# A second pair as seven products, with its sums stored early and another pair's sums made by transfers

## The chip, the cores and the metric

The kernel runs on one core of a Trainium2 chip. The metric is the time of one execution on the device in microseconds (us). Engines are named PE (TensorE, matmuls), PEld (TensorE's weight loads), DVE (VectorE), ACT (ScalarE), POOL (GpSimd) and SP (SyncE, which issues most transfers).

## What is computed

One decoder layer on 512 tokens of width 1024, all in float32: attention with forget gates, a residual with layer norm, a gated MLP with a causal convolution of three taps, a second residual with layer norm, and a gated embedding of 256 values per token.

```python
mix = fox_mixer(x, attn_w_in[j], attn_b_f[j], attn_w_out[j])
x = layer_norm(DEEPNORM_ALPHA * x + mix, ln_mix_g[i], ln_mix_b[i])
ffn = conv_ffn(x, ffn_w_up[i], ffn_conv_w[i], ffn_conv_b[i], ffn_w_down[i])
x = layer_norm(DEEPNORM_ALPHA * x + ffn, ln_ffn_g[i], ln_ffn_b[i])
gate = jax.nn.sigmoid(x @ ple_w_gate[i] + ple_b_gate[i])
x = x + gate * (p[i] @ ple_w_proj[i])
...
def conv_ffn(x, w_up, conv_w, conv_b, w_down):
    u, g = jnp.split(x @ w_up, [FFN_DIM], axis=-1)
    g = causal_dwconv(g, conv_w, conv_b)
    return (jax.nn.gelu(g, approximate=False) * u) @ w_down
```

The change lies in the MLP's first matrix product, `x @ w_up`, with 2 x 2816 output columns: 22 blocks of 128 for `g` and as many for `u`.

## The kernel before, in words

**Three matmuls for one.** Each float32 operand is cut into a high part, rounded to the matmul's type, and a low part, the rest. A product of two operands is the sum of three matmuls: high by high, high by low, low by high (`three`, L151). So a product of 128 x 1024 weights with 512 tokens is 8 row blocks of 3 matmuls, 24 in all.

**Weight units.** All weights pass through the class `Weights`, 128 x 1024 values at a time, called units, in the order in which they were added. A unit is loaded by SP into one of four `raw` tiles (or a spare part of the tile `side`, at places that a small loop fixes, L353 to 359); ACT makes its high part `whi` (L130); DVE makes its low part `wlo` by subtracting (L136). For units with `by_dma`, ACT instead writes the negated high part into `wlo` (L132), and POOL issues a transfer that adds the weights from DRAM to what lies there (L133). Pairs `whi` and `wlo` rotate in five places (`SPLIT_BUFS`), so the cut of a unit waits until TensorE is done with the one five back. A product asks for its unit with `get`, which also cuts up to four units ahead.

**Pairs.** The 22 blocks of features are worked through as eleven pairs, numbered 0 to 10. A plain pair (0, 1 and 10 before) is four products of 24 matmuls with 512 columns: `g` and `u` of each of its two blocks. A pair of seven products (`UP_PAIRS`) treats the 2 x 2 blocks of weights (two halves of the rows, two blocks of columns) by Strassen's scheme in Winograd's form: seven products of a quarter's size in place of eight, for `g` and `u` each, all with 256 columns (half of the tokens). `up_step` runs them in four steps, each for `g` and then for `u`: steps 0 to 2 have 24 matmuls a side, step 3 has 12. Steps 1 and 2 need sums of the weights' blocks and sums of the MLP's input, `xs`, which `x_sums` makes when pair 0 ends (L879 to 886). In step 0 ACT copies a half of the bank out and fills it with zeros (L913, L914), and step 1 adds to it; after step 1 ACT copies results into `E` (L922 to 925), after step 2 DVE subtracts (L929), and the convolution, Gelu and product of each block follow (L855 to 864).

**Where the weights' sums come from.** For `KEPT` pairs DVE makes them during the attention phase, and they are stored in DRAM as `kept` (`keep_load`, `keep_sums`, L544 to 547). For the pair in `IN_DRAM` the weights are copied to `kept` early (`up_copies`), and eight transfers of 256 KB that add within DRAM make the sums (`sums_beside`): ACT writes one value (L320), POOL copies it (L321) and issues the transfer (L322), one at each place that `BESIDE` names for a pair. After them come 16 such transfers for the sums of the last stage's gate weights. For the other pairs, 2 and 9, DVE makes the sums as their units arrive (L215, L216, L223, L237).

**Order.** From pair 1 on, ACT and DVE run in the order in which the code is written (`manual_schedule`). Each of the first three groups of three pairs is followed by its part of the second matrix product, spread over the pairs of the next group; pairs 0 to 2 have no such work beside them.

Of the kernel before, what the change touches and what calls it, by code (L numbers as in the profile page):

```python
# [12 lines left out]
AF = mybir.ActivationFunctionType  # L13
# [3 lines left out]
P = 128  # L17
# [13 lines left out]

CHUNKS = (None,) + ((1,) * 8 + (0, 1, 2, 1),) * 2 + ((1, 1, 2, 1, 2, 2, 2, 1),)

UP_PAIRS = (2, 3, 4, 5, 6, 7, 8, 9)

KEPT = (3, 4, 5, 6, 7)

IN_DRAM = (8,)

BESIDE = {2: (0, 2, 3), 3: (0, 2, 3), 4: (0, 2, 3), 5: (0, 2), 6: (0, 2, 3), 7: (0, 2), 8: (0, 2, 3),  # L40
          9: (0, 2, 3), 10: (0, 2)}

DMA_PAIRS = (1, 2)

APART = (2, 3, 4, 5, 6, 7, 8, 9)
HALF = S // 2
ALPHA = 2.0 ** 0.25
EPS = 1e-5
# [9 lines left out]
RAW_BUFS = 4  # L58

COPIES = (2, 3)  # L60

BANKS = ("six", "six", "two", "six", "six", "six", "two", "six")
SPLIT_BUFS = 5
# [86 lines left out]
def trunk_layer(ctx: ExitStack, tc: tile.TileContext, xT, x2d, pT, w0, wqk, wv1, wv2, bf, wo, wup, cwb,  # L150
                wdn, wpl, wg, bg, gm, bm, gf, bff, out):  # L151
    nc = tc.nc
# [21 lines left out]
    W = Weights(tc, base)  # L174
# [78 lines left out]
    def up_units(j):  # L253

        f0, f1 = 2 * j, 2 * j + 1
        if j in KEPT + IN_DRAM:
            return (lambda q: W.add(wup[f0, 1 - q], inner=P),
                    lambda q: W.add(kept[j, q][:, 0:4:3, :], inner=512),
                    lambda q: W.add([(kept[j, q][:, 2, :], 512), (wup[f1, 1 - q][:, 4:], 512)]),
                    lambda q: W.add([(kept[j, i][:, 1, :], 512) for i in range(2)]))  # L260

        def unit(f, q, make=None):
            return W.add(wup[f, 1 - q], inner=P, make=make, by_dma=make is None and j in DMA_PAIRS)

        add = nc.vector.tensor_add
        return (lambda q: unit(f0, q), lambda q: unit(f1, q, t12(wup[f0, 1 - q][:, :4], 3 + q, add)),
                lambda q: unit(f1, q, up_t3),
                lambda q: W.add([(wup[f0, 1 - i][:, 4:], 512) for i in range(2)], make=t4(3, op=add)))

    dram = ctx.enter_context(tc.tile_pool(name="dram", bufs=1, space=bass.MemoryType.DRAM))  # L270
    kept = {(j, q): dram.tile([P, 4, 512], F32, name=f"kept{j}_{q}")
            for j in KEPT + IN_DRAM for q in range(2)}

# [18 lines left out]
    def up_copies():  # L292

        for j in IN_DRAM:
            for q in range(2):
                for n in range(2):
                    nc.sync.dma_start(kept[j, q][:, 2 * n:2 * n + 2, :].rearrange("p a (k b) -> p (a k) b", b=P),
                                      wup[2 * j + n, 1 - q])
                    yield

    def sums_beside():

        def blocks(j):
            for to, src in ((0, None), (2, None), (3, 0), (1, 3)):
                for q in range(2):
                    t = kept[j, q]
                    if src is None:
                        yield (t[:, to, :].rearrange("p (k b) -> p k b", b=P),
                               wup[2 * j + 1, 1 - q][:, 2 * to:2 * to + 4])
                    else:  # L310
                        yield t[:, to, :], t[:, src, :]

        def gates():
            for to, src in (("t1", "b12"), ("t2", "t1"), ("t4", "t2"), ("t3", "b12")):
                for k in range(4):
                    yield quad(to, k, 1), quad(src, k, 1)

        for to, src in itertools.chain(*[blocks(j) for j in IN_DRAM], gates()):
            m = next(steps)
            nc.scalar.activation(small[:, m:m + 1], zeros[:, :1], AF.Copy)  # L320
            with tc.issue_after(nc.gpsimd.tensor_copy(small[:, m + 32:m + 33], small[:, m:m + 1]).ins):  # L321
                nc.gpsimd.dma_start(to, src, accum_op=ALU.add)  # L322
            yield

    u_up, u_dn = {}, [[] for _ in PAIRS]
    for part in range(4):
# [3 lines left out]
        for i in range(2 * len(fs)):  # L330
            f, q = fs[i // 2], i % 2
            j, n = f // 2, i % 4
# [20 lines left out]
    u = u_up[0, 1] + 5  # L353
    while u < len(W.units):
        spare(u, 5)
        both = u_up[2, 3, 0] < u + 3 < u_up[9, 1, 0] - 5
        if both:
            spare(u + 3, 3)
        u += 6 if both else 5
# [157 lines left out]


    to_keep = [(k, t) for k, t in kept.items() if k[0] in KEPT]
    in_work, made, last_sum, last_mask = [], [], [], []  # L520

    def keep_load(queue=nc.sync):

# [64 lines left out]
    def scores(h):  # L588
# [13 lines left out]
        off = 0  # L602
# [16 lines left out]
        off = 0  # L619
        for i in range(NT):  # L620
            w = (i + 1) * P
            nc.gpsimd.tensor_scalar_mul(pr[:, off:off + w], pr[:, off:off + w], rl[:, i:i + 1])  # L622
            off += w
        probs[h] = pr

# [80 lines left out]
    for h in range(H + 2):  # L706
# [3 lines left out]
        if h < H:  # L710
            scores(h)
            with tc.issue_after(last_mask[0]):
                for _ in range(2 if h in COPIES else 0):
                    next(copies)

            if s == 0 and h != 2:
                keep_sums()
                keep_load()
        elif s == 0:
            keep_sums()  # L720
            keep_load()
# [283 lines left out]
    before = None  # L1005
    pending = []
    beside = sums_beside()
    ordered = ExitStack()
    for part in range(4):
        ops = []  # L1010
# [1 line left out]

        def between():
            if next(place) in BESIDE.get(j, ()):
                next(beside)
            for _ in range(next(slots, 0)):
                next(before)

# [306 lines left out]
```

## Time and profile before

| | us |
|---|---|
| median of 3 runs | 642.45 (641.92 to 642.89) |
| the profiled execution | 642.98 |
| its span on the core | 641.3 |
| pair 0, first to last start of a matmul | 246.71 to 270.17 |
| pair 1 | 270.40 to 291.93 |
| pair 2 starts | 292.16 |

A line of the profile names an engine, a source line, an operation, and the tile written and read by the program's names, with the shape. In the timeline the two numbers ahead are start and duration in us; in brackets stands how long the engine was idle before it, and who released it. In a group the duration is in nanoseconds. The granted TensorE clock is full throughout. The page also shows these transfers that add, issued by POOL, with the kilobytes of each and the median time from issue to landing:

```profile
wlo<-wup POOLq DMA_DIRECT2D x6, 512.0 KB, 8.9
gt<-wg POOLq DMA_DIRECT2D x8, 256.0 KB, 7.2
gt<-gt POOLq DMA_DIRECT2D x8, 256.0 KB, 7.0
kept<-wup POOLq DMA_DIRECT2D x4, 256.0 KB, 7.8
kept<-kept POOLq DMA_DIRECT2D x4, 256.0 KB, 6.0
```

### The profile page before, as it was taken

Reading aid. Unit: us, or ns where it says so; the run is one execution under the profiler, and the core shown is the slowest. Engines: PE = TensorE matmul, PEld = TensorE weight load, DVE = VectorE, ACT = ScalarE, POOL = GpSimd, SP = SyncE. Lnnn points to the kernel's source line nnn. Section 1 sums busy time; section 2 is a strip of 40 time slices with the busy share of each in tenths; the row PEclk is TensorE's granted clock in tenths of the full one; section 3 lists DMA queues with packets and bytes.
Section 4 is the critical chain, followed back from the end, with each engine's and each line's share of the span. In section 5 each row is a group of like instructions: output and inputs, shape, how many; then the busy total and the mean of one; then the engine's idle time right before and its main releaser. Section 6 shows DMA issues by size and latency. Waiting matters only on the chain.

```text
span 641.3 us, 10471 instructions
## 1 busy us (share of the span) xinstructions
PE 635.4 (99%) x3780; PEld 566.2 (88%) x3780; DVE 545.9 (85%) x872; ACT 396.8 (62%) x716; POOL 135.8 (21%) x165
## 2 busy tenths in 40 slices
PE   9999999999999999999999999999999999999997
PEld 7899888888888889989999999999998998888886
DVE  6567779988888699857889989999898999699997
ACT  6264787877876326955766666757565745337772
POOL 2000464554456043110201110010011010002001
PEclk9999999999999999999999999999999999999999
DMA  8896634555678787695885778777769585672632
GB/s 315 279 320 210 225 111 141 189 177 157 205 261 308 262 258 221 142 253 153 209 244 171 206 240 230 229 205 205 218 193 273 155 203 159 180 262 64 228 112 99
DMA packets 54516, 132.66 MB, mean 207 GB/s; under 512 B 5376, under 2 KB 8448, under 8 KB 54464
## 3 DMA queue, kind: packets, MB, share of 16 engines
q1 hardware_dynamic: 48080, 115.60, 54.5%
q0 software_dynamic: 6240, 16.26, 13.3%
q8 instruction: 30, 0.49, 0.3%
q14 instruction: 22, 0.18, 0.1%
q10 hardware_dynamic: 144, 0.13, 0.1%
HBM read 117.16 MB, written 25.17 MB: 222 GB/s over the span
## 4 chain that ended last, share of the span: by engine, by line
PE 92%; DVE 3%; DMA 3%; ACT 1%; issue 1%; DVEq 0%; ACTq 0%; SPq 0%
PE g L159 16%; PE u L159 16%; PE pp L159 14%; PE pv L159 7%; PE x L159 7%; PE pl L159 7%; PE z L159 4%; PE ap L159 3%; PE r L159 3%; PE o L648 3%; PE t L635 2%; PE ao L159 2%; PE y L159 2%; PE s L598 2%; PE s L600 2%; DMA raw<-wdn 1%
## 5 line engine op out<-in xcount | busy, mean ns | idle before, releaser
L130 ACT ACTIVATE whi<-raw 128x1024 fp32r<-128x1024 f32 (+4 forms) x126 | 123.1, 980 | 86.2 <-PE pv L159 18.7
L136 DVE TENSOR_TENSOR wlo<-raw,whi 128x1024 fp32r<-128x1024 f32 (+4 forms) x121 | 134.8, 1121 | 22.3 <-ACT whi L130 22.0
L622 POOL TENSOR_SCALAR pr<-pr,rl 128x128 f32<-128x128 f32 (+1 forms) x64 | 75.7, 1200 | 74.6 <-DVE rl L618 74.6
L321 POOL COPY neghalf<-neghalf 128x1 f32<-128x1 f32 x24 | 9.2, 384 | 244.3 <-ACT neghalf L320 244.3
L159 PE MATMUL pp<-xh,whi 128*128 128x512 f32 (+1 forms) x130 | 50.8, 391 | 0.1
L159 PE MATMUL pp<-xl,whi 128*128 128x512 f32 (+1 forms) x130 | 50.8, 391 | 0.0
L159 PE MATMUL pp<-xh,wlo 128*128 128x512 f32 (+1 forms) x130 | 50.8, 392 | 0.0
L159 PE MATMUL g<-x1h,whi 128*128 128x256 f32 (+1 forms) x160 | 48.9, 306 | 0.8 <-ACT E L933 0.8
L159 PE MATMUL g<-x1l,whi 128*128 128x256 f32 (+1 forms) x160 | 48.7, 304 | 0.0
L159 PE MATMUL g<-x1h,wlo 128*128 128x256 f32 (+1 forms) x160 | 48.7, 304 | 0.0
L159 PE MATMUL u<-x1l,whi 128*128 128x256 f32 (+1 forms) x152 | 47.3, 311 | 0.0
L159 PE MATMUL u<-x1h,wlo 128*128 128x256 f32 (+1 forms) x152 | 47.3, 311 | 0.0
L159 PE MATMUL u<-x1h,whi 128*128 128x256 f32 (+1 forms) x152 | 47.2, 311 | 0.0
L136 DVE TENSOR_TENSOR wlo<-side,whi 128x1024 fp32r<-128x1024 f32 (+1 forms) x39 | 38.8, 1000 | 4.4 <-ACT whi L130 4.4
L130 ACT ACTIVATE whi<-side 128x1024 fp32r<-128x1024 f32 (+1 forms) x40 | 35.1, 883 | 11.1 <-PE u L159 3.4
L614 ACT ACTIVATE pr<-s,nm 128x128 f32<-128x128 f32 (+1 forms) x64 | 33.6, 528 | 11.9 <-DVE nm L610 11.7
L159 PE MATMUL g<-xsh,wlo 128*128 128x256 f32 x128 | 36.2, 283 | 0.0
L159 PE MATMUL u<-xsh,wlo 128*128 128x256 f32 x128 | 36.2, 283 | 0.0
L159 PE MATMUL u<-xsl,whi 128*128 128x256 f32 x128 | 36.2, 283 | 0.0
L159 PE MATMUL u<-xsh,whi 128*128 128x256 f32 x128 | 36.2, 283 | 0.0
L159 PE MATMUL g<-xsl,whi 128*128 128x256 f32 x128 | 36.2, 283 | 0.0
L159 PE MATMUL g<-xsh,whi 128*128 128x256 f32 x128 | 36.1, 282 | 0.0
(638 smaller groups left out, 1958.0 us busy)
## 6 DMA issues: line engine op xcount, KB each, us to landing
raw<-wup SPq DMA_DIRECT2D x27, 512.0 KB, 4.3
raw<-wdn SPq DMA_DIRECT2D x25, 512.0 KB, 4.8
raw<-wqk SPq DMA_DIRECT2D x14, 512.0 KB, 4.4
ka<-wup SPq DMA_DIRECT2D x10, 512.0 KB
kb<-wup SPq DMA_DIRECT2D x10, 512.0 KB, 3.5
kept<-kb SPq DMA_DIRECT2D x9, 512.0 KB, 3.9
kept<-ka SPq DMA_DIRECT2D x9, 512.0 KB
side<-wup SPq DMA_DIRECT2D x9, 512.0 KB, 6.0
```

What stands on the lines that cost most here:

```text
L130: self.nc.scalar.activation(hi[:, c:e], piece, AF.Copy)
L136: self.nc.vector.tensor_sub(lo[:, c:e], piece, hi[:, c:e].bitcast(F32))
L159: nc.tensor.matmul(ps, lhsT, rhs, start=start and n == 0, stop=stop and n == 2, skip_group_check=on)
L321: with tc.issue_after(nc.gpsimd.tensor_copy(small[:, m + 32:m + 33], small[:, m:m + 1]).ins):
L598: nc.tensor.matmul(ps[:, :n], QA[:, q], KA[:, :n], start=True, stop=False)
L600: nc.tensor.matmul(ps[:, :n], qb[0:68, q], kb[0:68, :n], start=False, stop=True)
L614: nc.scalar.activation(pr[:, off:off + w], ps[:, :w], AF.Exp, bias=nm[:, i:i + 1], scale=-1.0, accum_out=ls[:, i:i + 1])
L622: nc.gpsimd.tensor_scalar_mul(pr[:, off:off + w], pr[:, off:off + w], rl[:, i:i + 1])
L635: nc.tensor.transpose(ps[:, w:w + P], pr[:, o:o + P], ident)
L648: nc.tensor.matmul(ps[:, q0:], V[:, j, h], p[:, o:o + w], start=j == 0 and n == 0, stop=j == NT - 1 and n == 1)
```

## The change

Pair 1 becomes a pair of seven products, with its sums stored in the attention phase. Pair 7, the eighth, loses that place: its weights are copied to DRAM by SP, and its sums are made by eight transfers that add. Pair 8's copies move to POOL, in heads 5, 7, 9 and 11, each behind the head's last scaling (`COPIES_LATE`). `BESIDE` now names 1, 3 and then 4 places a pair, 32 transfers in place of 24: pair 7's from pair 2 to pair 4, pair 8's in pairs 5 and 6, the gate's 16 in pairs 7 to 10. Kept pairs that are in `DMA_PAIRS` make the low parts of their steps 0 and 1 by transfer, which is four units of pair 1; pair 2's step 0 does so before and after. The places of `side` as a spare buffer shift.

```diff
-UP_PAIRS = (2, 3, 4, 5, 6, 7, 8, 9)
-KEPT = (3, 4, 5, 6, 7)
-IN_DRAM = (8,)
-BESIDE = {2: (0, 2, 3), 3: (0, 2, 3), 4: (0, 2, 3), 5: (0, 2), 6: (0, 2, 3), 7: (0, 2), 8: (0, 2, 3),
-          9: (0, 2, 3), 10: (0, 2)}
+UP_PAIRS = (1, 2, 3, 4, 5, 6, 7, 8, 9)
+KEPT = (1, 3, 4, 5, 6)
+IN_DRAM = (7, 8)
+BESIDE = {2: (0,), 3: (0, 2, 3), 4: (0, 1, 2, 3), 5: (0, 1, 2, 3), 6: (0, 1, 2, 3), 7: (0, 1, 2, 3), 8: (0, 1, 2, 3), 9: (0, 1, 2, 3), 10: (0, 1, 2, 3)}
 DMA_PAIRS = (1, 2)
-APART = (2, 3, 4, 5, 6, 7, 8, 9)
+APART = (1, 2, 3, 4, 5, 6, 7, 8, 9)
 COPIES = (2, 3)
+COPIES_LATE = (5, 7, 9, 11)
...
-            return (lambda q: W.add(wup[f0, 1 - q], inner=P),
-                    lambda q: W.add(kept[j, q][:, 0:4:3, :], inner=512),
+            return (lambda q: W.add(wup[f0, 1 - q], inner=P, by_dma=j in DMA_PAIRS),
+                    lambda q: W.add(kept[j, q][:, 0:4:3, :], inner=512, by_dma=j in DMA_PAIRS),
...
-                    nc.sync.dma_start(kept[j, q][:, 2 * n:2 * n + 2, :].rearrange("p a (k b) -> p (a k) b", b=P),
-                                      wup[2 * j + n, 1 - q])
+                    queue = nc.sync if j == IN_DRAM[0] else nc.gpsimd
+                    queue.dma_start(kept[j, q][:, 2 * n:2 * n + 2, :].rearrange("p a (k b) -> p (a k) b", b=P),
+                                    wup[2 * j + n, 1 - q])
...
-        both = u_up[2, 3, 0] < u + 3 < u_up[9, 1, 0] - 5
+        both = u_up[2, 3, 0] + 6 < u + 3 < u_up[9, 1, 0] - 6 or u + 3 > u_up[9, 3, 0] + 6
...
-            nc.gpsimd.tensor_scalar_mul(pr[:, off:off + w], pr[:, off:off + w], rl[:, i:i + 1])
+            last_scale[:] = [nc.gpsimd.tensor_scalar_mul(pr[:, off:off + w], pr[:, off:off + w],
+                                                         rl[:, i:i + 1]).ins]
...
+            if h in COPIES_LATE:
+                with tc.issue_after(last_scale[0]):
+                    next(copies)
```

On ACT, where pair 1 begins, before: `whi_3011` and `wlo_3012` are the third product's unit of pair 1, `whi_3016` and `wlo_3017` the fourth's, `whi_3021` the first of pair 2.

```order
L130 ACTIVATE whi_3011<-side 128x1024
L132 ACTIVATE wlo_3012<-side 128x1024
L130 ACTIVATE whi_3016<-raw_2785 128x1024
L863 ACTIVATE a_2937<-a_2937 128x512
L132 ACTIVATE wlo_3017<-raw_2785 128x1024
L130 ACTIVATE whi_3021<-raw_2817 128x1024
L959 ACTIVATE a0h<-E_2741 128x512
L959 ACTIVATE b0h<-E_2741 128x256
L959 ACTIVATE s0h<-E_2741 128x1024
```

The same place on ACT in the changed kernel: `whi_3008` and `wlo_3009` are step 1 of pair 1 for `g`, `whi_3013` and `wlo_3014` for `u`, `whi_3018` is step 2.

```order
L130 ACTIVATE whi_3008<-side 128x1024
L132 ACTIVATE wlo_3009<-side 128x1024
L869 ACTIVATE a_2944<-a_2944 128x512
L130 ACTIVATE whi_3013<-raw_2791 128x1024
L132 ACTIVATE wlo_3014<-raw_2791 128x1024
L130 ACTIVATE whi_3018<-raw_2823 128x1024
L919 ACTIVATE side<-g_3007 128x256
L920 ACTIVATE g_3007<-zeros 128x256
L130 ACTIVATE whi_3056<-raw_2954 128x1024
L919 ACTIVATE side<-u_3055 128x256
```

The two cuts with a negated copy stand in the same order, the Gelu of pair 0 (`a`) moved ahead of the second, and the copy and the zeroing of pair 1's banks are new behind them.

On POOL, the transfers that finish low parts, before (four of pair 1, two of pair 2, then the first step for pair 8's sums):

```order
L133 DMA wlo_2813<-wup 128x1024
L133 DMA wlo_2943<-wup 128x1024
L133 DMA wlo_3012<-wup 128x1024
L133 DMA wlo_3017<-wup 128x1024
L133 DMA wlo_3022<-wup 128x1024
L133 DMA wlo_3065<-wup 128x1024
L321 COPY neghalf<-neghalf 128x1
```

And in the changed kernel, at the same place of POOL (`kept_0_63` and `kept_1_64` are pair 1's stored sums, `kept_0_73` is pair 7's):

```order
L133 DMA wlo_2819<-wup 128x1024
L133 DMA wlo_2950<-wup 128x1024
L133 DMA wlo_3009<-kept_0_63 128x2x512
L133 DMA wlo_3014<-kept_1_64 128x2x512
L133 DMA wlo_3136<-wup 128x1024
L133 DMA wlo_3170<-wup 128x1024
L323 COPY neghalf<-neghalf 128x1
L324 DMA kept_0_73<-wup 128x512
```

There are six as before, and the third and fourth now read stored sums.

On PE, where the second product of pair 1 ends and the third begins in the changed kernel (`u_3055` is pair 1's bank for `u`, `xs` the sums of the input, `h` and `l` high and low):

```order
L159 MATMUL u_3055<-x1h,whi_2949 128x256
L159 MATMUL u_3055<-x1l,whi_2949 128x256
L159 MATMUL u_3055<-x1h,wlo_2950 128x256
L159 MATMUL g_3007<-xsh,whi_3008 128x256
L159 MATMUL g_3007<-xsl,whi_3008 128x256
L159 MATMUL g_3007<-xsh,wlo_3009 128x256
```

Before, the same place reads like this, with the whole 512 tokens and no sums:

```order
L159 MATMUL g_3010<-x1h,whi_2812 128x512
L159 MATMUL g_3010<-x1l,whi_2812 128x512
L159 MATMUL g_3010<-x1h,wlo_2813 128x512
L159 MATMUL u_3061<-x1h,whi_2942 128x512
L159 MATMUL u_3061<-x1l,whi_2942 128x512
```

The third matmul of a group is the first that reads the low part.

More of the change, by code (lines that the diff above doesn't have):

```diff
@@ L316, in gates @@
                     yield quad(to, k, 1), quad(src, k, 1)
+        seen = yield
         for to, src in itertools.chain(*[blocks(j) for j in IN_DRAM], gates()):
             m = next(steps)
-            nc.scalar.activation(small[:, m:m + 1], zeros[:, :1], AF.Copy)
+            nc.scalar.activation(small[:, m:m + 1], zeros[:, :1] if seen is None else seen, AF.Copy)
             with tc.issue_after(nc.gpsimd.tensor_copy(small[:, m + 32:m + 33], small[:, m:m + 1]).ins):
                 nc.gpsimd.dma_start(to, src, accum_op=ALU.add)
-            yield
+            seen = yield
     u_up, u_dn = {}, [[] for _ in PAIRS]
@@ L519, in trunk_layer @@
     to_keep = [(k, t) for k, t in kept.items() if k[0] in KEPT]
-    in_work, made, last_sum, last_mask = [], [], [], []
+    in_work, made, last_sum, last_mask, last_scale = [], [], [], [], []
     def keep_load(queue=nc.sync):
@@ L1007, in trunk_layer @@
     beside = sums_beside()
+    next(beside)
     ordered = ExitStack()
@@ L1014, in between @@
             if next(place) in BESIDE.get(j, ()):
-                next(beside)
+                beside.send(None)
             for _ in range(next(slots, 0)):
```

## The prediction, made before the changed kernel ran

> **What bounds the kernel now.** I read the page's first part, then who waited for whom on TensorE, then its timeline around the second pair.
>
> ```profile
> span 641.3 us, 10471 instructions
> PE 635.4 (99%) x3780; PEld 566.2 (88%) x3780; DVE 545.9 (85%) x872; ACT 396.8 (62%) x716; POOL 135.8 (21%) x165
> PE 92%; DVE 3%; DMA 3%; ACT 1%; issue 1%; DVEq 0%; ACTq 0%; SPq 0%
> ```
> ```profile
> PE g L159 <- ACT E L933: 0.8, 1, 0.8
> PE warm L385 <- PEq L1316: 0.8, 1, 0.8
> ```
>
> TensorE is busy for 99% of the span and carries 92% of the chain that ended last. Its list of waits has two entries, 0.8 us each. So the kernel takes what its matmuls take, and a change pays only by removing matmul time, and only while weights arrive as fast as TensorE uses them. Ends of matmuls are modelled, so I count from start to start:
>
> ```profile
> 270.40 0.39 PE L159 MATMUL g<-x1h,whi 128*128 128x512 f32 x1
> ...
> 292.16 0.28 PE L159 MATMUL g<-x1h,whi 128*128 128x256 f32 x1
> ...
> 303.67 0.28 PE L159 MATMUL g<-xsh,whi 128*128 128x256 f32 x1
> ```
>
> The first row opens the second pair (pair 1), the next pair 2, the last pair 2's third step. Pair 1 is 4 products of 24 matmuls, 96 of 512 columns, in 292.16 - 270.40 = 21.76 us. Pair 2 already runs as seven products: its first two steps have four groups of 24 matmuls of 256 columns, of which 96 take 303.67 - 292.16 = 11.51 us, 0.120 us each, 2.88 us a group.
>
> **The change part by part.** *Seven products in pair 1.* They are 7 x 24 = 168 matmuls of 256 columns: 168 x 0.120 = 20.2 us in place of 21.76. This removes **1.6 us**, the only time that the change takes from the bound. Without stalls, the groups of pair 1 would start at 270.40, 273.28, 276.16 and 279.04, then two more of 2.88 and two halves of 1.44, and pair 2 at 290.56.
>
> *The four low parts by transfer.* Each group multiplies high weights, high weights, low weights, in that order for each of its eight row blocks, so its third matmul, 0.24 us after its start, needs the low part. For pair 1's first four groups ScalarE writes the high part and a negated copy, POOL issues a transfer that adds the weights, and TensorE waits for its landing. Before, the same four issues served four products of 5.4 us; now they serve groups of 2.88 us. ScalarE's two rows for the third, and POOL's first four issues:
>
> ```profile
> 266.87 1.05 ACT L130 ACTIVATE whi<-side 128x1024 fp32r<-128x1024 f32 x1
> 267.82 1.05 ACT L132 ACTIVATE wlo<-side 128x1024 fp32r<-128x1024 f32 x1
> ```
> ```profile
> 251.89 0.96 POOL L133 DMA_DIRECT2D wlo<-wup  x1 [0.27 <-issue]
> 262.88 0.87 POOL L133 DMA_DIRECT2D wlo<-wup  x1 [10.03 <-ACT wlo L132]
> 269.22 0.87 POOL L133 DMA_DIRECT2D wlo<-wup  x1 [5.47 <-ACT wlo L132]
> 271.69 0.86 POOL L133 DMA_DIRECT2D wlo<-wup  x1 [1.59 <-DVE E L864]
> ```
> ```profile
> DMA to landing us min/median/max: 7.8/8.9/10.0
> ```
>
> The last row is for the six such transfers. The rows of order above show ScalarE's work up to the third low part unchanged, and the fourth behind the same work (one Gelu goes ahead of it instead of into its middle), so I keep both issue times. The first two land by 251.89 + 10.0 = 261.9 and 262.88 + 10.0 = 272.9, before 273.28. The third, issued at 269.22, lands at the median at 278.1; TensorE wants it at 276.16 + 0.24 = 276.40: **a wait of 1.7 us**. The 22 matmuls left take 2.64, so the fourth is wanted at 278.1 + 2.64 + 0.24 = 281.0; it was issued at 271.69, close behind the third, so I give it the slowest landing, 281.7: **0.7 us** more. Together 2.4. At 7.8 us for both it is 0.6; at 10.0 for both 2.8, and I allow one us more, because the source is now the stored sums in pieces of 2 KB, of which no transfer into such a part is in the trace. I take 2.4, since nothing lightens the traffic there:
>
> ```profile
> 270.00:292.00 22.00, 22.00 (x99) 18.22 (x98) 13.49 (x21) 11.76 (x17) 2.66 (x4) 1.00 0.84 217
> 269.00:282.00 13.00, 13.00 (x59) 10.74 (x59) 7.47 (x12) 9.90 (x14) 3.44 (x4) 1.00 0.93 227
> ```
>
> (Stretches: busy us of PE, PEld, DVE, ACT, POOL, then granted clock, DMA share, GB/s.) From 269 to 282 the DMA engines are 93% busy already. Behind a waiting TensorE matmul stands everything, as it is the bound. The Trainium skill prices this otherwise: DMA: Bandwidth & Descriptors, in Anatomy of one DMA — SWDGE (gpsimd) path, fits such a transfer as 2.0 us plus its bytes over 436 KB per us, an estimate of 3.2 us for these 512 KB, and by it neither group would wait and the sum would keep all of the 1.6. The row's minimum of 7.8 speaks against it; those six add to what lies in place and meet other traffic.
>
> *Pair 2's two low parts.* They are made by transfer before and after, but five pairs of weight tiles turn, so a low part starts only when the group five back is done. ScalarE first makes three copies of that group's results (0.83 us here, from the first row to the fourth), then the two cuts and POOL's issue (269.22 - 266.87 = 2.35).
>
> ```profile
> 304.52 0.39 ACT L922 ACTIVATE E<-u 128x256 f32<-128x256 f32 x1
> 304.78 0.40 ACT L923 ACTIVATE E<-u 128x256 f32<-128x256 f32 x1
> 305.05 0.44 ACT L925 ACTIVATE E<-side 128x256 f32<-128x256 f32 x1
> 305.35 0.22 ACT L320 ACTIVATE neghalf<-zeros 128x1 f32<-128x1 f32 x1
> ```
>
> Pair 1's fourth group ends at 281.7 + 2.64 = 284.3; plus about 0.2 to notice, 0.83, 2.35 and 8.9 is 296.6. TensorE wants it four groups on, at 284.3 + 11.52 + 0.24 = 296.1: **0.5 us** (0 at 7.8, 1.6 at 10.0). The one before comes at 278.1 + 2.64 + 12.28 = 293.0 for 293.2: nothing.
>
> *VectorE and ScalarE around pair 1.* Three low parts by VectorE (1.22 us), four sums more of 0.4 to 0.7: some 5.9 us, beside the 8.5 us that VectorE idles from 270 to 292. The sums of the MLP's input for the third group were last made at 264.6 to 265.8, over 10 us early. Bank zeroing for pair 2's third group I read at pair 2's end:
>
> ```profile
> 309.63 0.69 DVE L929 TENSOR_TENSOR E<-E,u 128x512 f32<-128x512 f32 x1
> ```
> ```profile
> 317.14 0.39 ACT L914 ACTIVATE g<-zeros 128x256 f32<-128x256 f32 x1
> 264.59 1.22 DVE L886 TENSOR_TENSOR xsl<-x1t3l,xsh 128x1024 fp32r<-128x1024 f32 x1
> ```
>
> That is 317.53 - 309.63 = 7.9 us, and VectorE has about 0.7 more in it at pair 1's end: 8.6, where TensorE leaves three groups, 8.64. Nothing, with up to 0.5 if it slips.
>
> *Pair 7's sums and the gate's.* Pair 7 gives its stored sums of the attention phase to pair 1, so VectorE's work there is the same; eight more transfers of 256 KB add sums in DRAM, and the gate's 16 come later. Each costs ScalarE 0.19 us and POOL an issue.
>
> ```profile
> L322 POOL DMA_DIRECT2D kept<-kept x4: 807/812/831, 331.2 to 364.1; - x4
> DMA to landing us min/median/max: 4.9/7.0/10.8
> ```
> ```profile
> 490.44 1.06 ACT L130 ACTIVATE whi<-raw 128x1024 fp32r<-128x1024 f32 x1 [2.03 <-DMA raw<-wdn]
> ```
> ```profile
> 435.00:464.00 29.00, 29.00 (x201) 27.04 (x200) 26.62 (x36) 18.41 (x30) 2.36 (x4) 1.00 0.75 213
> 464.00:492.00 28.00, 27.16 (x199) 25.72 (x199) 24.51 (x35) 17.78 (x32) 3.96 (x6) 1.00 0.80 222
> ```
>
> The DMA engines have 20 to 25% left there, which hides them; where cover was gone, at 490.44, ScalarE waited 2.03 us for weights and TensorE 0.8 for ScalarE. I take **0.3 us**, between -0.8 (that stall goes) and +2. Four more copies of 512 KB in the attention phase are issued by POOL after a head's last scaling, beside its idle time, so nothing:
>
> ```profile
> L622 POOL TENSOR_SCALAR pr<-pr,rl 128x128 f32<-128x128 f32 (+1 forms) x64 | 75.7, 1200 | 74.6 <-DVE rl L618 74.6
> ```
>
> **Sum:** -1.6 + 2.4 + 0.5 + 0.3 = **+1.6 us**. The profiled execution took 642.98 (the span and 1.7 around it), so it would take 644.6. It lies 0.5 above the median of the runs, 642.45, so a median of **644.1**.
>
> **The rivals.** *The transfers land in time* (the other side). If the third and fourth land within 7.0 us, the median of the accumulating transfers of half their size, they are there at 276.2 and 278.7, before 276.40 and 279.28, and the whole 1.6 stays: 640.9, or 640.1 with the stall at 490 gone. It decides below about 7.2 us. For it: TensorE finds pair 2's transfers out of the busiest stretch now. Against it: six landings, none under 7.8. The page's 3.2 us ends here too. Chance 0.20.
>
> *A draw*: both land in 7.8, so 0.6 waits, pair 2 loses nothing, traffic costs 0 to 1: 641.5 to 642.5, up to 643.5 with part of pair 2's wait. Chance 0.17.
>
> *Traffic becomes the bound*: pairs 5, 7 and 10 go from two to four transfers beside them, and loads queue in SP's order behind a late one. Two or three stalls like that at 490, with 2 us each, or the third and fourth transfer a us later each: 646 to 648. For it the 93%, against it the 20% left later. Chance 0.13.
>
> *The stored sums come too late*, so that SP's queue stops at a load: pair 7's last sum is issued in pair 4 and pair 8's in pair 6, a whole pair of some 30 us ahead of the loads, against landings of at most 10.8. Its price would be several us; I leave it inside the last chance. That the change doesn't do what it says is excluded by the rows of order: the groups are 256 wide, with the sums.
>
> **How the numbers follow.** Forecast 0.50, with its own range 643.0 to 645.6. A measurement of this kernel tells about 0.2%, 1.3 us, from no change, so faster means below 641.2 and slower above 643.7. Faster: the first rival, 0.20. Same: the draw and a fifth of the forecast, 0.27. Slower: the rest, 0.53. The range of 640.3 to 647.0 reaches into the first and the third rival and leaves out less than 2 in 10.
>
> **What would show it.** TensorE's waits should have two new entries in pair 1, for low parts filled from the stored sums, 1 to 3 us together, perhaps one at pair 2's second group; pair 1 should take 22 to 23 us from its first matmul to pair 2's first. No such entry and a pair of 20.2 us would prove me wrong in the landing; a pair 1 as forecast and waits from 370 on would prove the traffic underpriced.

## The result and the profile after

| | before | after |
|---|---|---|
| median of 6 runs, us | 642.40 (641.92 to 642.89) | 651.41 (649.62 to 652.90) |
| the profiled execution, us | 642.98 | 652.34 |
| its span, us | 641.3 | 650.6 |

The ratio is 1.0132, with a 95% interval of 1.0115 to 1.0149: the changed kernel is slower by 9 us, outside the range of 640.3 to 647.0, where the forecast was slower by 1.6. The two profiled executions differ by 9.36 us. Three of the experiments below have one execution that was far slower (892 us in e6, 3583 in e12, 896 in e14); the ratios leave it out, the medians count it.

The first part of the page of the changed kernel, and its chain of work that ended last:

```profile
span 650.6 us, 10671 instructions
PE 636.6 (98%) x3852; PEld 570.2 (88%) x3852; DVE 551.1 (85%) x879; ACT 404.1 (62%) x739; POOL 156.5 (24%) x185
PE 84%; DVE 6%; issue 5%; DMA 4%; ACT 1%; POOL 0%; SPq 0%; DVEq 0%; POOLq 0%; ACTq 0%
```

TensorE carries 84% of that chain, not 92%, so something now stops it. Who waited for whom on PE (total, times, longest, in us):

```profile
PE u L159 <- DMA wlo<-kept: 5.4, 1, 5.4
PE g L159 <- DVE side L924: 1.3, 1, 1.3
PE u L159 <- DVE side L924: 0.9, 1, 0.9
PE g L159 <- DMA wlo<-kept: 0.8, 1, 0.8
PE warm L387 <- PEq L1323: 0.8, 1, 0.8
PE g L159 <- ACT E L939: 0.3, 1, 0.3
```

Four entries are new. The two `wlo<-kept` are pair 1's third and fourth low part, as forecast, but the fourth costs 5.4 us; the two on the tile `side` are in pair 2 and were not forecast. The old wait on `E` shrank from 0.8 to 0.3. ScalarE's row for the fourth's negated copy, POOL's timeline of the third and fourth transfer, and a summary of the landings of all six:

```profile
269.41 1.05 ACT L132 ACTIVATE wlo<-raw 128x1024 fp32r<-128x1024 f32 x1
```
```profile
268.46 1.21 POOL L133 DMA_DIRECT2D wlo<-kept  x1 [5.54 <-ACT wlo L132]
276.81 1.19 POOL L133 DMA_DIRECT2D wlo<-kept  x1 [7.14 <-DMA wlo<-kept]
```
```profile
DMA to landing us min/median/max: 7.2/7.9/8.9
```

The transfers are not slower than before (7.8/8.9/10.0). The third is issued at 268.46 and lands 8.0 us later; the fourth is issued only at 276.81, though ScalarE's negated copy for it ended at 269.41 + 1.05 = 270.46: POOL sat idle for 7.14 us until the third had landed. In the kernel before, the same two were issued 2.5 us apart, and three were outstanding at once. TensorE's timeline around the fourth, and stretches of the same time (busy us of PE, PEld, DVE, ACT, POOL, then granted clock, DMA share, GB/s):

```profile
276.55 0.39 PE L159 MATMUL g<-xsh,wlo 128*128 128x256 f32 x1 [0.85 <-DMA wlo<-kept]
...
285.09 0.58 PE L159 MATMUL u<-xsh,wlo 128*128 128x256 f32 x1 [5.40 <-DMA wlo<-kept]
285.47 0.41 PE L159 MATMUL u<-xsh,whi 128*128 128x256 f32 x1
285.69 0.41 PE L159 MATMUL u<-xsl,whi 128*128 128x256 f32 x1
...
291.21 0.28 PE L159 MATMUL g<-xsh,whi 128*128 128x256 f32 x1
...
306.34 0.39 PE L159 MATMUL g<-xsh,whi 128*128 128x256 f32 x1 [1.30 <-DVE side L924]
...
310.40 0.39 PE L159 MATMUL u<-xsh,whi 128*128 128x256 f32 x1 [0.93 <-DVE side L924]
```
```profile
280.00:285.00 5.00, 0.00 (x0) 0.00 (x0) 1.96 (x3) 2.48 (x5) 0.88 (x1) 0.93 1.08 230
285.00:291.00 6.00, 5.91 (x27) 5.91 (x28) 0.00 (x0) 0.81 (x3) 0.00 (x0) 0.50 0.68 147
291.00:296.00 5.00, 5.00 (x43) 5.00 (x42) 2.33 (x4) 3.91 (x6) 0.88 (x1) 0.98 0.37 107
```

From 285 to 291 the matmuls start 0.21 us apart in place of 0.12, with the granted clock at 0.50. That is a loss that no list of waits shows: from 285.09 to 291.21 the trace has 28 steps from one matmul to the next, 6.12 us where 28 x 0.120 = 3.36 is usual, so 2.76 are lost. Counted from start to start beyond the usual distance, the terms compare like this:

| term | forecast | trace after |
|---|---|---|
| pair 1's matmuls | -1.6 | -1.6 |
| wait for the third low part | 1.7 | 1.0 |
| wait for the fourth | 0.7 | 5.6 |
| half clock behind it | 0 | 2.76 |
| pair 2's second low part | 0.5 | 0 |
| pair 2's waits on `side` | 0 | 1.46 + 1.09 = 2.55 |
| traffic, the old wait on `E` | 0.3 | -0.6 |
| sum | 1.6 | 9.7 |

The two executions differ by 9.36: pair 1 began 0.85 us earlier in the second (269.55 for 270.40), and some 0.5 us of the difference are in none of the rows. Pair 1 took from 269.55 to 299.12, 29.6 us.

### The profile page after: what moved, and what is told of

Same layout as the page of the kernel before. It is cut to its first block, busy times and chain, and to the rows that moved or that the text cites. A ratio compares the mean times of both kernels' runs of the same rounds, so it can differ in the third digit from the quotient of the medians.

```text
span 650.6 us, 10671 instructions
## 1 busy us (share of the span) xinstructions
PE 636.6 (98%) x3852; PEld 570.2 (88%) x3852; DVE 551.1 (85%) x879; ACT 404.1 (62%) x739; POOL 156.5 (24%) x185
## 4 chain that ended last, share of the span: by engine, by line
PE 84%; DVE 6%; issue 5%; DMA 4%; ACT 1%; POOL 0%; SPq 0%; DVEq 0%; POOLq 0%; ACTq 0%
PE pp L159 14%; PE u L159 13%; PE g L159 12%; PE pv L159 7%; PE x L159 7%; PE pl L159 7%; PE z L159 3%; PE ap L159 3%; PE r L159 3%; PE o L651 3%; PE t L638 2%; PE ao L159 2%; PE y L159 2%; DVE wlo L136 2%; PE s L600 2%
## 5 line engine op out<-in xcount | busy, mean ns | idle before, releaser
L136 DVE TENSOR_TENSOR wlo<-raw,whi 128x1024 fp32r<-128x1024 f32 (+4 forms) x123 | 138.0, 1128 | 24.8 <-ACT whi L130 24.5
L323 POOL COPY neghalf<-neghalf 128x1 f32<-128x1 f32 x32 | 21.1, 659 | 231.2 <-ACT neghalf L322 231.2
L159 PE MATMUL u<-xsh,wlo 128*128 128x256 f32 x144 | 42.0, 292 | 5.4 <-DMA wlo<-kept 5.4
L159 PE MATMUL g<-x1l,whi 128*128 128x256 f32 (+1 forms) x156 | 45.8, 294 | 0.0
L159 PE MATMUL g<-x1h,wlo 128*128 128x256 f32 (+1 forms) x156 | 45.8, 294 | 0.0
L159 PE MATMUL u<-xsh,whi 128*128 128x256 f32 x144 | 41.8, 290 | 0.9 <-DVE side L924 0.9
L159 PE MATMUL g<-xsh,whi 128*128 128x256 f32 x144 | 41.0, 285 | 1.3 <-DVE side L924 1.3
L159 PE MATMUL g<-xsh,wlo 128*128 128x256 f32 x144 | 41.1, 285 | 0.8 <-DMA wlo<-kept 0.8
L159 PE MATMUL u<-xsl,whi 128*128 128x256 f32 x144 | 41.7, 289 | 0.0
L159 PE MATMUL g<-xsl,whi 128*128 128x256 f32 x144 | 41.0, 285 | 0.0
```

The costliest lines, as they stand in the source:

```text
L136: self.nc.vector.tensor_sub(lo[:, c:e], piece, hi[:, c:e].bitcast(F32))
L159: nc.tensor.matmul(ps, lhsT, rhs, start=start and n == 0, stop=stop and n == 2, skip_group_check=on)
```

## The experiments

Times are medians; ratios are against the kernel before, run on the same chip at the same time. Each edit is to the kernel after unless it says otherwise.

| run | us | before | ratio |
|---|---|---|---|
| e1_room_2048 | 649.45 | 641.89 | 1.0097 (1.0066 to 1.0129) |
| e2_one_piece | 646.18 | 641.89 | 1.0076 (1.0049 to 1.0102) |
| e3_sums_by_vector | 643.03 | 641.89 | 1.0030 (1.0008 to 1.0053) |
| e4_pair1_plain | 643.16 | 641.89 | 1.0019 (1.0008 to 1.0029) |
| e5_first_step_only | 645.49 | 642.30 | 1.0050 (1.0038 to 1.0063) |
| e6_all_by_vector | 645.11 | 642.30 | 1.0046 (1.0030 to 1.0061) |
| e7_before_room_512 (one run) | 664.62 | 642.30 | |
| e8_room_1152 (one run) | 652.13 | 642.30 | |
| e9_fourth_alone | 644.36 | 642.41 | 1.0030 (1.0018 to 1.0042) |
| e10_zeros_in_stall | 652.51 | 642.41 | 1.0178 (1.0146 to 1.0210) |
| e11_zeros_in_both | 650.11 | 641.73 | 1.0129 (1.0113 to 1.0144) |
| e12_second_by_vector | 646.97 | 641.73 | 1.0076 (1.0062 to 1.0089) |
| e13_lows_free | 643.03 | 641.79 | 1.0019 (1.0010 to 1.0027) |
| e14_before_lows_free | 642.55 | 641.79 | 1.0007 (0.9997 to 1.0017) |
| e15_no_sums_pair2 | 642.06 | 642.02 | 1.0009 (0.9995 to 1.0023) |
| e16_sums_on_pool | 645.55 | 642.02 | 1.0052 (1.0040 to 1.0065) |

### Why the fourth transfer was issued late

The kernel sets aside 1024 bytes of each partition for the descriptors of POOL's transfers. First that size alone was changed.

```diff
-dynamic_dma_scratch_size=1024
+dynamic_dma_scratch_size=2048
```

> The kernel after with 2048 in place of 1024 bytes of each partition set aside for POOL's transfers; nothing else changes. Theory A (room): POOL held the fourth of pair 1's low-part transfers from 270.46 (ACT's copy done) to 276.81 because the third, with two pieces of 2 KB per partition (256 in all), was still outstanding and both don't fit at once; with twice the room the fourth is issued at 270 to 272, lands at 280 to 282, PE's wait for it shrinks from 5.4 to 1 to 2 us, the granted clock doesn't fall to 0.50 behind it, and pair 2's waits on VectorE's side tile go: 643 to 645 us. Theory B (the wait is one between the instructions, or the queue takes transfers of this kind one at a time): the issue stays at 276.8 and the time at 650 to 652 us.

POOL's timeline of this run, the third and fourth:

```profile
269.04 1.21 POOL L133 DMA_DIRECT2D wlo<-kept  x1 [5.60 <-ACT wlo L132]
271.46 1.19 POOL L133 DMA_DIRECT2D wlo<-kept  x1 [1.20 <-ACT wlo L132]
```

The issue moved to 271.46, so theory A holds for the issue and B falls: no wait between instructions was touched. The time followed only in part, to 649.45 where 643 to 645 was expected. Side by side the two landed late, at 278.82 and 283.81, and the third, which had cost 0.8, now cost 2.6:

```profile
278.86 0.39 PE L159 MATMUL g<-xsh,wlo 128*128 128x256 f32 x1 [2.57 <-DMA wlo<-kept]
283.85 0.39 PE L159 MATMUL u<-xsh,wlo 128*128 128x256 f32 x1 [0.36 <-DMA wlo<-kept]
```

Behind it the clock was at half again, for 3.4 us, and pair 2's waits on `side` did not go (0.6 and 0.9 us), which the expectation had put down to the stall. From pair 1's first matmul to the one behind the first of these waits it took 302.43 - 270.14 = 32.29 us, against 306.34 - 269.55 = 36.79 in the kernel after, so 4.5 us were gained; 2.1 of them went again near 497, where TensorE's wait on `E`, behind a late load of weights, was 2.4 us in place of 0.3:

```profile
PE g L159 <- ACT E L939: 2.4, 1, 2.4
```

The second run kept 1024 bytes and halved the pieces.

```diff
-W.add(kept[j, q][:, 0:4:3, :], inner=512, by_dma=j in DMA_PAIRS)
+W.add(kept[j, q][:, 1:3, :] if j == 1 else kept[j, q][:, 0:4:3, :], inner=UNIT if j == 1 else 512, by_dma=j in DMA_PAIRS)
...
-queue.dma_start(to[:, 2 * n:2 * n + 2, :], t.rearrange("p (a b) -> p a b", b=512))
+rows = slice(1 - n, 4 - n, 2) if to is kept.get((1, 0)) or to is kept.get((1, 1)) else slice(2 * n, 2 * n + 2)
+queue.dma_start(to[:, rows, :], t.rearrange("p (a b) -> p a b", b=512))
```

> The kernel after, with the four stored blocks of pair 1 in another order in DRAM, so that the two that the second step takes lie side by side: a transfer has one piece of 4 KB per partition (128) in place of two of 2 KB (256). The same bytes, the same instructions. Theory A (room counted in pieces): both fit, the fourth is issued at 270 to 272 and the time is 642.5 to 645 us, as with more room. If the room were counted in bytes, or the queue took transfers from stored blocks one at a time: 650 to 652 us, issue at 276.8.

```profile
269.12 0.86 POOL L133 DMA_DIRECT2D wlo<-kept  x1 [5.47 <-ACT wlo L132]
271.59 0.85 POOL L133 DMA_DIRECT2D wlo<-kept  x1 [1.60 <-ACT wlo L132]
```

The same bytes, stored side by side, and both are outstanding together: the room counts pieces, not bytes. An issue also costs POOL 0.86 us in place of 1.21. The time came down to 646.18, above the 642.5 to 645 expected: by PE's list the two still cost 1.1 and 1.0 us, and pair 2's waits on `side` 1.3 and 0.9. Two more runs bracket the room: the kernel before with half of it, and the kernel after with an eighth more.

```diff
-dynamic_dma_scratch_size=1024
+dynamic_dma_scratch_size=512    (e7, the kernel before)
+dynamic_dma_scratch_size=1152   (e8, the kernel after)
```

> The kernel before with 512 in place of 1024 bytes of each partition for POOL's transfers; nothing else changes. Theory A (room by pieces: in the kernel before three transfers of 128 pieces were outstanding at 275.31, and two of 256 didn't fit in the kernel after; so 1024 bytes hold between 27 and 33 pieces and completions on each of 16 engines): 512 bytes hold one transfer of 9 but not two, each of POOL's transfers waits until the one before has landed, the fourth is issued at 277 to 278 in place of 271.69 and the fifth and sixth 8 us apart, and PE waits for the later ones: 646 to 665 us. If the room plays no part: the issue times and the time stay, 641 to 643 us.

> The kernel after with 1152 in place of 1024 bytes for POOL's transfers. A transfer of 256 pieces puts 16 pieces and one completion on each of 16 engines; two make 34. If the room is 32 bytes for each (16 to read and 16 to write), 1024 bytes hold 32 and 1152 hold 36: the fourth is issued at 270 to 272, as with 2048 bytes, and the time is that of 2048 bytes, 645 to 651 us. If more than that is needed: still at 276 to 277.

POOL in the unchanged computation with 512 bytes, the third, fourth and fifth:

```profile
284.11 0.87 POOL L133 DMA_DIRECT2D wlo<-wup  x1 [7.17 <-PE u L159]
291.70 0.86 POOL L133 DMA_DIRECT2D wlo<-wup  x1 [6.72 <-DVE a L858]
299.17 0.87 POOL L133 DMA_DIRECT2D wlo<-wup  x1 [6.60 <-issue]
```

With 512 bytes even the transfers of 128 pieces go one at a time, 7.5 us apart, each as the one before lands. The releasers named there (PE, DVE, issue) had long been done: for a wait on room the profile names whatever came last. The run was 22 us slower; some 12 of these fell ahead of the MLP, where the gate's transfers held up POOL's own work for the layer norm, so the fourth's issue, expected at 277 to 278, came at 291.70. With 1152 bytes the fourth was issued at 271.83:

```profile
271.83 1.22 POOL L133 DMA_DIRECT2D wlo<-kept  x1 [1.20 <-ACT wlo L132]
```

That run was no faster, all the same (the fourth landed at 282.69 and cost 2.6, and a late load of weights cost 2.6 more on `E` near 498). So 1024 bytes hold three transfers of 128 pieces but not two of 256, and 1152 hold those two. The trace has 256 packets of 2 KB and 16 of 4 bytes for the one kind, 128 of 4 KB and 16 of 4 bytes for the other. At 32 bytes a packet, spread over the 16 DMA engines, two of the large kind need 2 x 17 x 32 = 1088 bytes, three of the small kind 864 and two 576, which fits all four sizes. The 32 bytes are an inference: counted so, the runs leave anything from 1024/34 = 30.1 to 1152/34 = 33.9 bytes a packet. The Trainium skill, DMA: Bandwidth & Descriptors, section SWDGE vs HWDGE vs iDMA, has POOL write descriptors into rings that lie in a reserved part of SBUF; that a full ring holds the issue back is an inference from it, with which these four runs agree.

### What the wait costs beyond itself

Forty matmuls with weights of zero were put where PE sat idle, then 10 and 36 in both waits.

```diff
+if (j, st, s, col, k) == (1, 1, 1, 0, 0):    (e11: for both s)
+    for wt, x in ((hi[:, w], mh), (hi[:, w], ml), *[(zero, one)] * 40, (lo[:, w], mh)):    (e11: 36 if s else 10)
+        nc.tensor.matmul(to, wt, x, start=False, stop=False, skip_group_check=True)
+    continue
```

> The kernel after, with 40 more matmuls of 256 columns with weights of zero (they add nothing to the sums) on PE between the second matmul of pair 1's last unit of the second step and the third, which waits for the fourth transfer: the 5.4 us in which PE sat idle hold 4.3 to 4.8 us of work. The transfer lands when it did, so PE's useful work goes on at the same point. Theory C (the half clock from 284.7 to 291.1 comes from PE sitting idle): the granted clock stays at 1.00 there, the 23 matmuls of 285 to 290 that took 0.21 us apiece take 0.12, and the time falls by 2.5 to 3.2 us, to 648.2 to 649.5 us. Theory D (these matmuls are slow for another reason, such as the transfers' traffic): no change, 650.5 to 653 us.

> The kernel after, with matmuls with weights of zero in both of pair 1's waits: 10 (1.2 us) ahead of the matmul that waits for the third transfer, 36 (4.2 us) ahead of the one that waits for the fourth. In the run with 40 in the fourth's wait alone the third came 2.5 us later, PE sat idle for 3.4 us there, the clock fell for 3.4 us behind that wait, and the fourth landed before the 40 were through; behind the filled wait the clock stayed at 1.00. Theory C (idle PE sets the clock): with no gap over 2 us the clock stays at 1.00 through 275 to 300 and the time is 648 to 650 us. If the third is late by over 3 us again, a half clock shows behind its gap alone: 650 to 652.5 us. Theory D (half clock from something else): the clock falls behind the filled wait too, 651 to 654 us.

The first was spoiled as a measure of time: its third low part landed 10.5 us after its issue, so PE sat idle there for 3.4 us, and the 40 matmuls outlasted the fourth's landing by 2 us. Its clock is still telling; stretches behind the idle gap and within and behind the filled one:

```profile
281.40:284.30 2.90, 2.90 (x13) 2.90 (x14) 2.87 (x4) 0.25 (x1) 1.19 (x1) 0.50 0.29 74
285.60:290.00 4.40, 4.40 (x43) 3.85 (x41) 0.00 (x0) 2.84 (x5) 0.88 (x1) 1.00 0.77 206
290.00:294.00 4.00, 4.00 (x37) 4.00 (x35) 0.00 (x0) 1.12 (x4) 0.00 (x0) 1.00 0.82 196
```

The second had no idle gap over 1.72 us in pair 1, and no half clock:

```profile
286.30 0.37 PE L918 MATMUL u<-xsh,wlo 128*128 128x256 f32 x1
...
304.80 0.39 PE L159 MATMUL g<-xsh,whi 128*128 128x256 f32 x1 [1.35 <-DVE side L932]
```
```profile
280.00:286.00 6.00, 6.00 (x55) 5.52 (x54) 3.11 (x4) 3.17 (x6) 1.38 (x2) 1.00 0.79 173
286.00:291.00 5.00, 5.00 (x45) 4.96 (x43) 0.00 (x0) 1.81 (x5) 0.37 (x1) 1.00 0.96 201
```

Theory C holds and D falls: the same matmuls behind the same wait run at full speed once PE was kept busy. From the matmul that the fourth released to the next wait it took 304.80 - 286.30 = 18.50 us, against 306.34 - 285.09 = 21.25 in the kernel after: 2.75 us, beside the 2.76 worked out above. The whole time fell by less, to 650.11, and the trace doesn't account for that: it is of an execution of 652.89 us, the slowest of the four, in which pair 1 began 1.15 us later than in the kernel after (270.70 for 269.55) and the wait on `E` near 500 took 2.3 us in place of 0.3. The third landed 9.9 us after its issue here (8.0 in the kernel after) and the fourth 6.4 (8.2), so that the fourth released TensorE 15.60 us after pair 1's start, against 15.54. Why the landings differ between runs was not tried.

### What is left when the fourth is mended

Four ways to take the third transfer, or the third and fourth, out of pair 1's path (e3, e5, e6, e9), and pair 1 plain with everything else as after (e4).

```diff
-W.add(kept[j, q][:, 0:4:3, :], inner=512, by_dma=j in DMA_PAIRS)
+W.add(kept[j, q][:, 0:4:3, :], inner=512)                                    (e3, e5)
+W.add(kept[j, q][:, 0:4:3, :], inner=512, by_dma=j in DMA_PAIRS and q == 1)  (e9)
-DMA_PAIRS = (1, 2)
+DMA_PAIRS = (1,)    (e5)
+DMA_PAIRS = ()      (e6)
...
-UP_PAIRS = (1, 2, 3, 4, 5, 6, 7, 8, 9)
+UP_PAIRS = (2, 3, 4, 5, 6, 7, 8, 9)    (e4; APART likewise)
-KEPT = (1, 3, 4, 5, 6)
+KEPT = (3, 4, 5, 6)    (e4)
```

> The kernel after, with VectorE making the low parts of pair 1's second step (two subtractions of 128x1024) in place of the third and fourth transfer; the other four transfers stay. If the whole loss sits behind these two transfers: PE's waits of 1.0 and 5.4 us, the slow clock and pair 2's late side tiles go, and what is left is the gain of the 24 matmuls of 512 columns' worth, 641 to 642 us. If another part of the change costs as well (traffic beside the pairs, the zeroing of PSUM): 643 to 646 us. If VectorE is now late for pair 1's sums, a new wait of 1 to 2 us on a low part or on the side tile shows there.

> The kernel after, with pair 1 plain as in the kernel before (its stored blocks gone too, so attention has four pairs to store, not five); the eighth pair's and all the gate's sums stay with the transfers beside the MLP. If the transfers beside the pairs are covered: 641.5 to 643 us, as before. If their traffic costs (the rival with a price of 3 to 5 us): 645 to 648 us, with losses spread over parts 1 to 3.

> The kernel after with only the two transfers of pair 1's first step left: VectorE makes the low parts of pair 1's second step and of pair 2's first step (four subtractions of 128x1024 at 1.22 us). With the second step's alone moved to VectorE, pair 2's transfers were issued at 283.29 and 286.08 (in the kernel before: 275.31 and 279.12) and cost PE 0.5 and 1.4 us. Theory: a look-ahead counted in units is worth half as much time once a unit holds 24 matmuls of 256 columns in place of 512, so any 8 to 9 us transfer of these pairs is late; without them the 1.9 us go and the time is 640.5 to 641.8 us. Rival: VectorE, which had 4.9 of 5 us busy in places here, is now late with the sums (side tile, E) by more than that: 643 to 645 us.

> The kernel after with no low part by a transfer: VectorE makes all six (six subtractions of 128x1024 at 1.22 us). ACT saves six negated copies, POOL six issues. In the 10 us before 260 VectorE is busy for 9.93, so the two low parts of pair 1's first step come on top there. If that stretch is the limit: 2.4 us of VectorE work become about as much PE wait near 255 to 268, 642.5 to 645 us. If there is slack: as with the first step by transfers, within 1 us.

> The kernel after, with VectorE making the third low part (one subtraction of 128x1024 at 1.22 us) and the fourth still by a transfer of 256 pieces, now with no other of its size beside it. Room: it fits, so it is issued at 269 to 272, lands in 8 us alone at 277 to 280, and is wanted at 279 to 280; the third is no wait (in the run with both by VectorE there was none). So PE's waits in pair 1 sum to 0 to 1 us and the clock stays at 1.00; what is left are pair 2's 1.9 to 2.5 us of waits on its transfers or on VectorE: 642.5 to 645 us. If a single transfer of two pieces per partition were late by itself: a wait of 2 us or more in pair 1 and 645 to 648 us.

The stall is worth some 7 to 8 us: e3 (643.03) and e9 (644.36, its fourth issued at 270.21 with a wait of 0.2) come down from 651.41 to 0.3% above before. None goes below it. In e3 PE waits for pair 2's transfers instead:

```profile
PE u L159 <- DMA wlo<-wup: 1.2, 1, 1.2
PE warm L387 <- PEq L1323: 0.8, 1, 0.8
PE u L159 <- DVE side L924: 0.4, 1, 0.4
PE g L159 <- DMA wlo<-wup: 0.4, 1, 0.4
```

These transfers are issued at 283.29 and 286.08, in the kernel before at 275.31 and 279.12. Their lead is a number of units, and a unit of pair 1 now lasts 2.88 us in place of 5.44; with e5 this was to be repaired, but the rival came true: VectorE was late by 2.0 us on `side`, with a half clock of 3.4 us behind that. e6 showed the same 2.0 in the same place, and none of the waits near 255 to 268 that it was to show. In e4 PE's list is that of before but for 0.4 us more on `E` and two waits of 0.2 to 0.3, and the time is 0.2% up: the other parts of the change cost about 1 us; 643.16 lies just above the first sum of its expectation. Where the rest of that lies its trace doesn't show.

### Who eats the 1.6 us

Then the six transfers were left out altogether, in the kernel after and in the kernel before.

```diff
-self.nc.gpsimd.dma_start(lo[:, c:e].rearrange("p (a b) -> p a b", b=inner), src, accum_op=ALU.add)
```

> The kernel after without the six transfers that add the weights to the negated copies (so the low parts of pair 1's first two steps and of pair 2's first step stay negated copies; left out of the computation), and without any work in their place; TensorE's matmuls are all there. If the loss is all in how the low parts are made: no wait on a low part, no half clock, and the time is below the kernel before by the 1.6 us of matmuls less 0 to 1 us of traffic (with pair 1 plain and the other parts as after, the time was 0.2% above the kernel before): 640.5 to 642 us. If VectorE's added sums or the zeroing of PSUM in pair 1 cost by themselves: a wait on a side tile of 1 to 2 us at pair 2's second step remains, 642.5 to 644 us.

> The kernel before without its six transfers of low parts (left out of the computation in the same way). If they are covered there, as its trace shows (PE waits for none of them): 641.5 to 642.5 us, no difference from the kernel before. If taking 12 transfers' worth of traffic away between 252 and 289 frees something else: up to 1 us less.

e14 is level with before: its transfers were covered. In e13 pair 1 takes 269.91 to 290.06, 20.15 us, so the matmuls' gain is there; and yet 643.03. PE's list, and VectorE's timeline ahead of the wait (a line number is two lower in this kernel):

```profile
PE g L157 <- DVE side L922: 1.3, 1, 1.3
PE u L157 <- DVE side L922: 0.9, 1, 0.9
```
```profile
284.57 0.69 DVE L933 TENSOR_TENSOR E<-E,g 128x512 f32<-128x512 f32 x1 [2.22 <-PE g L157]
...
294.45 0.69 DVE L868 TENSOR_TENSOR E<-a,E 128x512 f32<-128x512 f32 x1 [0.76 <-ACT a L867]
295.06 0.68 DVE L227 TENSOR_TENSOR side<-side 128x512 f32<-128x512 f32 x1
295.66 1.22 DVE L134 TENSOR_TENSOR wlo<-raw,whi 128x1024 fp32r<-128x1024 f32 x1
296.80 0.42 DVE L922 TENSOR_TENSOR side<-g,side 128x256 f32<-128x256 f32 x1
```

The two waits are those of the kernel after, to 0.1 us. VectorE works from 284.57 to 297.22 with one gap of 0.76 and reaches `side` 1.3 us late. In the kernel before it stood idle ahead of the same instruction:

```profile
296.06 0.42 DVE L918 TENSOR_TENSOR side<-g,side 128x256 f32<-128x256 f32 x1 [1.21 <-ACT g L914]
```

A plain pair gives its blocks one after the other, and the convolution and product of each fit beside the next one's matmuls. Seven products give all results at the end, and this work stands in one row ahead of pair 2's `side`. The last runs took work out of that row, or moved it.

```diff
+same = lambda t: None if t is None else [t]                  (e15, with e13's edit: pair 2's units with no sums made)
+nc.gpsimd.tensor_add(t[:, :512], t[:, 512:], t[:, :512])     (e16, with e5's: two of pair 2's sums)
-if amid is not None:                                         (e12, with e3's: operand sums behind side in pair 2,
+if amid is not None and j != 2:                               and pair 2's second low part by VectorE)
```

> The kernel after without the six transfers of low parts and without VectorE's additions that make pair 2's weight sums (left out of the computation: pair 2's sums are plain blocks, the low parts negated copies; TensorE's matmuls are all there). In the run without the transfers VectorE was busy from 284.57 to 297.22 without a gap but one of 0.76 us, and PE waited for the end of it; of that stretch 2.75 us are such additions, and 1.22 us more stand ahead of the second wait. If VectorE's work there is what eats the gain: both waits (1.3 and 0.9 us) go, and the time falls from 643.0 to 640.4 to 641.2 us, below the kernel before. If another wait takes their place (ACT's E, the zeroing): 642 to 643 us.

> The kernel after with VectorE making pair 1's second-step and pair 2's low parts (four subtractions; two transfers stay), and with two of pair 2's additions (128x512, 0.69 us each on VectorE) on POOL, which has nothing else to do there. Without the move this kernel was at 645.5 us, with a wait of 2.0 us on the side tile in pair 2 and a half clock of 3.4 us behind it. If POOL makes each in 4 us or less: the wait shrinks to 0.6 to 0.8 us, the clock stays at 1.00 and the time is 641.8 to 643.5 us. If POOL's addition takes longer than ACT can wait for: a new wait on a high part, 645 us or more.

> The kernel after, with VectorE making pair 1's two second-step low parts and the second of pair 2's first step (its transfer cost PE 1.36 us with pair 1's by VectorE; VectorE sat idle for 2.2 us where the subtraction now stands), and with the sums of pair 1's operands one instruction later for pair 2, behind the side tile on which PE waited 0.6 us. Three transfers stay. If these waits are what is left of the loss: the waits behind 285 shrink from 2.5 to 0.5 to 1 us and the time is 641 to 642.3 us, level with the kernel before. If VectorE is the limit in pair 2 whatever the order: a new wait of 1 to 2 us on a side tile or E, 643 to 645 us.

e15's list shows what is left of these waits:

```profile
PE g L157 <- DVE side L926: 0.5, 1, 0.5
PE u L157 <- DVE side L926: 0.3, 1, 0.3
```

The first is pair 2's, down from 1.3 us, and pair 2's second wait is gone; the 0.3 stands at 504, in pair 9. So it is VectorE's work that makes pair 2's waits, though not all of the first went. The time went from 0.19% above the kernel before to 0.09%, which is level with it; the two intervals overlap, and it did not go below before as expected. The traces show where the gain goes: from pair 0's first matmul to pair 9's, e15 takes 243.7 us for 245.1 before, but from there to the last matmul of the MLP 70.3 for 69.1. From 500 to 524 VectorE is busy for 23.67 of 24 us in both, and e15's waits there, 0.3 on `side` and 0.2 on `y`, are on VectorE. That it takes the gain back in pair 9 is read from the trace, and no run tests it. e16 and e12 missed: POOL made each sum in at most 2.24 us, but the two waits on `side` stayed at 1.1 and 0.9 and a new one of 1.5 us on `E` (VectorE again) stood ahead of them; in e12 the subtraction waited 2.3 us for ScalarE instead of falling into VectorE's gap, and everything on VectorE was later by that. No version ran faster than the kernel before.

## Why the prediction was wrong, point by point

- *What bounds the kernel, and the gain.* Right. Pair 1 without stalls is 20.15 us, forecast 20.2.
- *The third low part.* Right in kind: 1.0 us, forecast 1.7, with a landing after 8.0 us in place of the median of 8.9.
- *The fourth.* This step failed. It kept "both issue times" from the order of ScalarE's work and gave the fourth 271.69. ScalarE was indeed ready, at 270.46. The text had noted that the source is now "in pieces of 2 KB" and allowed one us more for the landing; the pieces acted on the issue instead. e1, e2, e7 and e8 show that two transfers of 256 pieces don't fit in 1024 bytes: the issue came 5 us later than assumed, and the wait was 5.6 us, not 0.7.
- *What stands behind a waiting TensorE.* The text has "everything, as it is the bound" stand there, and priced it at the length of the wait. The half clock behind it added 2.76 us; e11 measured 2.75.
- *VectorE and ScalarE around pair 1.* This step failed too. It set 5.9 us of work against 8.5 us of idle time over the whole pair, and followed one chain to the end of ScalarE's zeroing (7.9, with 0.7 more), where TensorE leaves 8.64. The wait ended on VectorE's addition behind that, which stood in a row of 12.65 us. It costs 1.46 + 1.09 us in the kernel after, and within 0.1 us as much in e2 and e13, whether there is a stall or not; e15 ties it to VectorE's work.
- *Pair 2's low parts.* No wait in the kernel after, in part by luck: the second landed in 7.2 us where 8.9 was taken. In e3 the two cost 1.6 by PE's list, against 0.5.
- *The traffic.* Forecast 0.3, between -0.8 and 2; e4 puts all other parts of the change at about 1.2 us (0.5 to 1.9). The stall on `E` behind a late load, 0.8 us before, took 0.3 in the kernel after, 2.3 to 2.6 in e1, e8 and e11, and isn't listed in e2, e3 and e13; what sets it was not tried.
- *The rivals.* None names the mechanism. "The third and fourth transfer a us later each" came nearest, with one us for the fourth where 5 came. With the fourth mended, the change is a loss of 1.1 to 1.9 us (e3, e9), near the forecast's 1.6, though made of other terms.

## What to carry to other kernels

Before two transfers issued by GpSimd are taken to overlap, count their pieces against the memory set aside for their descriptors: a rearranged source can double the pieces and turn two overlapping transfers into two in a row. When TensorE is the bound, price a stall with the slow stretch that follows it. And idle time of a helper engine over a whole stage doesn't hide added work: look at the row of instructions ahead of the one that TensorE waits for.

## What the runs showed of the hardware

- *Room for POOL's transfers.* 512 bytes of a partition held one transfer of 128 pieces at a time, 1024 three of them but only one of 256, 1152 two of 256. POOL's issue took 0.86 us for 128 pieces and 1.21 for 256.
- *Two transfers side by side.* 512 KB in 256 pieces, with no other of that size beside it, landed 8.0 and 8.2 us after the issue in the kernel after and 8.8 in e9, but 10.5 and 6.2 in e10 and 9.9 and 6.4 in e11. Of two side by side the first landed after 9.8 and the second after 12.3 in e1, and after 7.5 and 10.9 in e8; with 128 pieces each, after 8.2 and 9.9 (e2).
- *The clock.* By the record of the granted clock, half speed came, among the matmuls, in stretches of 3.4 us (one in e1, e5, e6, e8, e10 and e7) or of 6.8 (one in the kernel after and one in e7). Such a stretch went with a distance between matmul starts of 2.25 us (e6), 2.26 (e5), 2.83 (e8), 2.85 (e1), 3.49 (e10), 4.35 and 6.25 (e7) and 5.68 (after); others of 2.55 (e11), 2.65 (e1), 2.92 (e8), 3.39 and 3.84 (e7) had none, nor had any up to 1.9. So the gap alone doesn't decide. The Trainium skill, TensorE: Matmul & The Clock Gate, section Part 1: The HAM clock gate, gives a free-running window of about 3.4 us and half speed after an idle one; the stretches agree with that length, while gaps of 2.25 us are shorter than such a window.
